# Paced splits of w_out, layer-norm statistics from sums and squares for three tiles, and a last unit in whole steps

## The chip, the cores and the metric

The kernel runs on one core of a Trainium2 chip. The metric is the device time of one launch in microseconds. TensorE multiplies matrices, VectorE and GpSimd work element by element, ScalarE applies functions, SyncE issues most of the loads. TensorE's clock has two levels, 1.2 and 2.4 GHz, and the profile gives the granted share of the higher one.

## The reference

One layer of a decoder trunk over 512 tokens of 1024 features, in float32. What matters here is the end of the first half and the second half:

```python
merged = sigmoid(mg_h) * (o_h @ w_br_hg) + sigmoid(mg_n) * (o_n @ w_br_nsa)
y = (1 + g1) * (merged @ w_out)
x = layer_norm(ALPHA * x + y) * ln1_g + ln1_b
h = layer_norm(x) * (1 + sc2) + sh2
y = (1 + g2) * hier_moe(h, ...)     # top-1 group of 4, top-2 of its 8 experts, 32 experts of 1024 x 512
x = layer_norm(ALPHA * x + y) * ln2_g + ln2_b
```

`layer_norm` takes the mean and the mean of the squared distances from it over the 1024 features of a token, with 1e-5 under the root.

## The kernel before

The 512 tokens are four tiles of 128. Until about 625 us the input projection, the two mixing branches and their gates are worked off. Every float32 matrix product there is made of three passes: each operand is split into a rounded high part and the rest (`wh` and `wl` of a weight, `mh` and `ml` of the merged activations), and high by high, high by low and low by high are summed in PSUM.

`run_jobs` (L332) goes through a list of jobs. A job has a weight block and a body that yields every few matmuls. At each yield the generator `ahead` (L336) is stepped once: it splits one piece of a coming block. `split1` issues for a piece the rounding on ScalarE (L279, `wh`) and the difference on VectorE (L281, `wl`); for the blocks of `w_out`, which are marked early, VectorE first scales the piece by 1 + g1 (L270). Each of the two `w_out` blocks is 512 columns wide and has four pieces. The block that is next is split first; of the three blocks after it, those marked early follow. Each engine works off its instructions in the order in which they were issued.

The jobs around the change are, in order: four blocks of `w_br_hg`, four of `w_br_nsa` (`br_job`, 256 columns each, 48 matmuls each into two PSUM tiles `pbr`), and the two of `w_out` for the first tile. For each `pbr` of `w_br_nsa` VectorE forms the gated sum (L1090, L1094), ScalarE rounds it (L1096, `mh`) and VectorE takes the rest (L1097, `ml`). There are eight of these groups, one for each 128 features of the merged activations.

`out_piece` (L1120) multiplies the merged activations of a tile by `w_out`, half a row at a time, adds ALPHA times the input row (L1126, `z`) and takes BN_STATS of the half (L1128). `ln` (L1199) then runs for each tile: BN_AGGR (L230) gives mean and variance, ScalarE's Ln and Exp (L232, L233) the reciprocal root `rs`; VectorE forms `acc` = (z - mean) x gain (L1207) and, by halves, `acc` x rs + bias (L1213) with BN_STATS of the result (L1214), from which a second BN_AGGR, Ln and Exp give the statistics `l2` of the norm ahead of the experts. TensorE transposes `z`, ScalarE copies it out (`zT`, L1222) and TensorE forms the router's logits from it (`plg`, L1194 and around). The router's choices on VectorE (`pk`, L1232 to L1262) lead to the ranks `prk` on TensorE and to the gather lists; the normed row `xh` (L1239) is split into `xhh` (L1242, ScalarE) and `xhl` (L1244, GpSimd for tiles 0 to 2; L1286, VectorE, within the last tile's gather). The work of the tiles is interleaved: each `yield` in `ln` is a due time for a planner that puts the next tile's `out_piece` in between. The last tile takes its BN_STATS in quarters and is ordered by hand.

The experts' weights come as 512 KB tiles `ew` on the queue of SyncE. L1315 issues them, each as its buffer comes free, in order. TensorE multiplies the gathered tokens (`p`, `py`, L182), and `pcb` (L180) adds the outcome back to the tokens' rows.

The last unit holds four experts side by side, each on 32 columns of TensorE. `half_up(h, py, ks)` issues the second product of half h of the output columns for the steps ks of the contraction, four instructions for each step. `weighted_halves` scales the product (L1541, `y`), rounds it (L1543, `yh`) and takes the rest (L1544, `yl`). `half_add` adds a tile's share to `acc` and sums the row (L1714); `squares` lets ScalarE sum the squares (L1697). `pl` spreads the gain and bias of the last norm over the partitions, ScalarE copies them out (L1737). Between the two halves' sums and the end stands `overflow`, a loop for tokens over an expert's 32 places that is not entered here, and a load of ScalarE's function table (L1749).

Of the kernel before, what the change touches and what calls it, by code (L numbers as in the profile page):

```python
# [26 lines left out]
AF = mybir.ActivationFunctionType  # L27
OP = mybir.AluOpType
# [39 lines left out]
LN_T, LN_P, LN_Q, LN_L, LN_R = 5000, 1500, 800, 0, 3500  # L68
MOD_F = 2
MOD_G = 2  # L70
SMALL = (8, 9)
# [68 lines left out]
def hybrid_kernel(ctx, tc, a, out, dbg=None, stop=None):  # L140
# [14 lines left out]
    def Q(name, dt=F32):  # L155
        return big.tile([128, 1024], dt, name=name, tag="Q", bufs=36)
# [163 lines left out]
    def run_jobs(jobs):  # L320
# [3 lines left out]
        def ahead(i):  # L324

            nb = [b for b in blocks[i + 1:] if b is not None]
            for b in nb[:1]:
                while len(b.w) < b.np:
                    b.fetch1()
                while len(b.h) < b.np and not b.raw:  # L330
                    b.split1()
                    yield  # L332
            for b in nb[1:4]:
                if b.early or b is nb[1]:
                    while len(b.w) < b.np:
                        b.fetch1()  # L336
                while b.early and len(b.h) < b.np:
                    b.split1()
                    yield
            while True:  # L340
                yield
# [778 lines left out]
    def out_piece(b, i, c, width):  # L1120

        z, n = zs[i], 256 if i + 1 == NT else 512
        py = PS("pyo")[:, 0:width]
        yield from proj_tok(b, py, i, mh, ml, width, c % 512)
        s_ = slice(c, c + width)
        V.scalar_tensor_tensor(z[:, s_], z[:, s_], ALPHA, py, op0=OP.mult, op1=OP.add)  # L1126
        for j in range(c // n, (c + width) // n):
            V.bn_stats(l1st[i][:, 6 * j:6 * j + 6], z[:, j * n:(j + 1) * n])  # L1128

# [58 lines left out]
    def logits_of(i):  # L1188
# [8 lines left out]
        return plg, lgT  # L1197

    def ln(i, z, st):  # L1199
        last = i == NT - 1  # L1200
        if last:
            tail_transposed()
            gather_first([0])
        mv, rs = layer_stats(z, "l1", st, later=True)
        ac = Q("acc")
# [5 lines left out]
        for half in range(2):  # L1211
            s_ = slice(half * 512, (half + 1) * 512)
            V.scalar_tensor_tensor(ac[:, s_], ac[:, s_], rs[:, 0:1], l1b[:, s_], op0=OP.mult, op1=OP.add)  # L1213
            V.bn_stats(st[:, half * 6:(half + 1) * 6], ac[:, s_])  # L1214
        mv2, rs2 = layer_stats(ac, "l2", st, later=True)
        if not last:
# [20 lines left out]

        xh = Q("xh")
        A.activation(xh.rearrange("p (k q) -> p q k", k=8), ac.rearrange("p (q k) -> p q k", k=8), AF.Identity,  # L1239
# [484 lines left out]
    py, py1 = PS("py"), PS("py")  # L1724
    for _ in half_up(0, py, range(4)):
        pass
    l2g, l2b = Q("l2g"), Q("l2b")
    pls = []
    for h_, l_ in zip(l2h, l2l):
        for s_ in halves_:  # L1730
            ps = PS("pl2")
            for j, x in enumerate((h_, l_)):
                mm(ps, oner, x[:, s_], j == 0, j == 1)
            pls.append(ps)
    y = weighted_halves(py, cs_, 0, 512)
    for j, ps in enumerate(pls):
        A.activation((l2g, l2b)[j // 2][:, halves_[j % 2]], ps, AF.Copy)  # L1737

    for x, _ in enumerate(half_up(1, py1, (0, 1))):
        if x < NT:  # L1740
            half_add(0, y, x)
    V.tensor_scalar(nsh, sums[:, :, 0], -1.0 / 512, None, op0=OP.mult)
    for _ in half_up(1, py1, (2, 3)):
        pass
    for i in range(NT):
        squares(i, 0)
    y = weighted_halves(py1, cs_, 512, 512)
    overflow()
    A.preload_act_table_set("natural_log_exp_and_others")  # L1749
    for i in range(NT):  # L1750
        half_add(1, y, i)
        squares(i, 1)
# [59 lines left out]
```

## Time and profile before

| | us |
|---|---|
| median of three runs | 1254.59 |
| the three runs | 1252.58 to 1255.31 |
| the profiled execution, whole time | 1251.85 |
| its span on the core | 1250.1 |
| TensorE busy in the span | 1171.4 (94%) |
| VectorE busy | 691.8 (55%) |
| ScalarE busy | 431.5 (35%) |
| GpSimd busy | 85.4 (7%) |

The times of the table and of the rows are of one profiled execution. Busy shares are means over stages with different limits: up to about 660 us TensorE is nearly always busy and the DMA engines little; from about 756 to 1217 us the DMA engines are; in between and behind, several engines wait for each other. Waits are given with what ended them. A line number is one of the kernel before; in the changed kernel the same statement stands 1 to 26 lines further down. Float32 matmuls are shown with their passes in some rows, so that 12 instructions can stand as 24.

### The profile page before, as it was taken

Reading aid. Unit: us, or ns where it says so; the run is one execution under the profiler, and the core shown is the slowest. Engines: PE = TensorE matmul, PEld = TensorE weight load, DVE = VectorE, ACT = ScalarE, POOL = GpSimd, SP = SyncE. Lnnn points to the kernel's source line nnn. Section 1 sums busy time; section 2 is a strip of 40 time slices with the busy share of each in tenths; the row PEclk is TensorE's granted clock in tenths of the full one; section 3 lists DMA queues with packets and bytes.
Section 4 is the critical chain, followed back from the end, with each engine's and each line's share of the span. In section 5 each row is a group of like instructions: output and inputs, shape, how many; then the busy total and the mean of one; then the engine's idle time right before and its main releaser. Section 6 shows DMA issues by size and latency. Waiting matters only on the chain. (4 is left out here: it accounts for less than half of the span.)

```text
span 1250.1 us, 18158 instructions
## 1 busy us (share of the span) xinstructions
PE 1171.4 (94%) x6455; PEld 803.1 (64%) x6455; DVE 691.8 (55%) x1626; ACT 431.5 (35%) x904; POOL 85.4 (7%) x164
## 2 busy tenths in 40 slices
PE   5999999899999999999998979999999899999986
PEld 4788898778888888878876763434435235455322
DVE  5564888787665665423495797535135134444314
ACT  4333656764444353555232341201102001112013
POOL 3011111121011011002000020000000000000000
PEclk9999999999999999999998989999999999999997
DMA  9954324134244244336255199999999999999991
GB/s 319 311 142 156 94 72 127 55 124 139 77 148 122 77 129 126 86 99 208 61 176 168 34 343 345 409 408 409 408 409 409 409 409 409 408 408 402 408 362 71
DMA packets 137629, 296.10 MB, mean 237 GB/s; under 512 B 11195, under 2 KB 74883, under 8 KB 137536
## 3 DMA queue, kind: packets, MB, share of 16 engines
q1 hardware_dynamic: 128224, 268.57, 58.9%
q0 software_dynamic: 8544, 23.97, 6.2%
q10 hardware_dynamic: 768, 2.37, 0.6%
q8 instruction: 52, 0.85, 0.3%
q14 instruction: 41, 0.34, 0.1%
HBM read 292.73 MB, written 4.76 MB: 238 GB/s over the span
## 5 line engine op out<-in xcount | busy, mean ns | idle before, releaser
L182 PE MATMUL p<-ew,xe 128*32 128x512 f32 (+1 forms) x960 | 195.6, 597 | 10.6 <-DMA ew<-in_exp_w_dram 10.1
L281 DVE TENSOR_TENSOR wl<-wst,wh 128x1024 fp32r<-128x1024 f32 (+1 forms) x93 | 109.6, 1201 | 75.4 <-ACT wh L279 74.5
L182 PEld LDWEIGHTS p<-ew,xe 128*32 128x32 f32 (+1 forms) x960 | 53.4, 122 | 146.1 <-issue 81.9
L182 PE MATMUL py<-ew,aT 128*32 128x512 f32 (+1 forms) x464 | 99.1, 598 | 8.8 <-DMA ew<-in_exp_w_dram 5.9
L1520 DVE TENSOR_TENSOR s<-s,p 128x512 f32<-128x512 f32 x13 | 8.9, 687 | 175.6 <-PE p L182 159.9
L279 ACT ACTIVATE wh<-wst 128x1024 fp32r<-128x1024 f32 (+1 forms) x94 | 93.9, 1031 | 32.7 <-DVE wst L270 20.2
L182 PEld LDWEIGHTS py<-ew,aT 128*32 128x32 f32 (+1 forms) x464 | 24.9, 121 | 73.6 <-issue 38.5
L1528 ACT ACTIVATE aT<-pat 128x512 f32<-128x512 f32 x13 | 7.8, 597 | 176.4 <-PE pat L186 176.4
L1569 DVE TENSOR_TENSOR acc<-acc,pcb 128x512 f32<-128x512 f32 x96 | 58.3, 681 | 8.3 <-PE pcb L180 8.3
L1543 ACT ACTIVATE yh<-y 128x512 fp32r<-128x512 f32 x26 | 16.4, 630 | 130.1 <-DVE y L1541 130.1
L180 PE MATMUL pgx<-pm,xhh 128*128 128x256 f32 (+1 forms) x224 | 55.6, 293 | 0.0
L180 PE MATMUL pgx<-pm,xhl 128*128 128x256 f32 (+1 forms) x224 | 54.1, 287 | 0.0
L1541 DVE SCALAR_TENSOR_TENSOR y<-py,cs,g2b 128x512 f32<-128x512 f32 x26 | 19.4, 748 | 58.5 <-PE py L182 58.3
L180 PE MATMUL pmg<-hh,wh 128*128 128x512 f32 x128 | 50.4, 394 | 0.0
L180 PE MATMUL psg<-hh,wh 128*128 128x512 f32 x128 | 50.3, 393 | 0.0
L180 PE MATMUL psg<-hl,wh 128*128 128x512 f32 x128 | 49.9, 390 | 0.0
L180 PE MATMUL psg<-hh,wl 128*128 128x512 f32 x128 | 49.9, 390 | 0.0
L180 PE MATMUL pmg<-hh,wl 128*128 128x512 f32 x128 | 49.8, 389 | 0.0
L180 PE MATMUL pmg<-hl,wh 128*128 128x512 f32 x128 | 49.8, 389 | 0.0
L180 PE MATMUL pcb<-yh,pT 128*128 128x512 f32 x104 | 44.0, 423 | 5.3 <-issue 5.3
L180 PEld LDWEIGHTS pgx<-pm,xhh 128*128 128x128 f32 x224 | 43.6, 197 | 8.0 <-issue 6.9
L519 POOL DMA_DIRECT2D adaw<-in_ada_w_dram x64 | 34.6, 542 | 193.4 <-PE ptp L186 40.2
(538 smaller groups left out, 2784.1 us busy)
## 6 DMA issues: line engine op xcount, KB each, us to landing
ew<-in_exp_w_dram SPq DMA_DIRECT2D x380, 512.0 KB, 10.1
wst<-in_w_in_dram SPq DMA_DIRECT2D x66, 512.0 KB, 4.8
adaw<-in_ada_w_dram POOLq DMA_DIRECT2D x64, 256.0 KB, 3.2
adaw<-in_ada_w_dram SPq DMA_DIRECT2D x16, 512.0 KB, 9.3
wst<-in_w_br_hg_dram SPq DMA_DIRECT2D x8, 512.0 KB, 6.8
wst<-in_w_br_nsa_dram SPq DMA_DIRECT2D x8, 512.0 KB, 3.6
wst<-in_w_out_dram SPq DMA_DIRECT2D x8, 512.0 KB, 6.7
ext_d<-ext_d POOLq DMA_DIRECT2D x1, 2560.0 KB, 17.1
```

The lines of the kernel that those rows point to most:

```text
L180: PE.matmul(o, l, r, start=start, stop=stop)
L182: PE.matmul(o, l, r, start=start, stop=stop, tile_position=pos)
L279: A.activation(wh, self.w[j], AF.Copy)
L281: (sub or V).tensor_sub(wl, self.w[j], wh.bitcast(F32))
L519: P_.dma_start(w, ada[:, k, 2048 + j * 512:2560 + j * 512])
L1520: V.tensor_mul(s1, s1, p3)
L1528: A.activation(aT, at_.rearrange("p (f s) -> p f s", f=4), AF.Copy)
L1541: V.scalar_tensor_tensor(y, py, cs_, g2b[c0 // 512][:, c0 % 512:c0 % 512 + n], op0=OP.mult, op1=OP.mult)
L1543: A.activation(yh, y, AF.Copy)
L1569: V.tensor_add(acc[i][:, s_], acc[i][:, s_], pc_)
```

## The change

There are three parts. First, `ahead` yields four times instead of once after each piece of an early block (`PACE = 4`), so that one piece of `w_out` is split in four steps. Second, for tiles 0 to 2 the statistics of both norms come from sums: L1126 and L1213 take an accumulated sum along with their result, a new `stats_of_sums` makes the mean of the two halves' sums on VectorE, and ScalarE takes the sum of the squares of mean - x over the whole row (its result goes to a buffer that later holds `xh`), then Ln and Exp. The last tile stays as it was. Third, in the last unit the steps run whole: the first half's steps 0 and 1, the eight `pl` with their copies, its steps 2 and 3, `weighted_halves`, then steps 0 and 1 of the second half, the four `half_add`, and steps 2 and 3 of the second half. Of the first half's squares only those of tiles 0 and 1 stay ahead of `yh`; those of tiles 2 and 3 follow behind the loop and the table load.

```diff
--- before.py
+++ after.py
@@ -67,6 +67,7 @@
 LOADS = [4, 4, 4, 4]
 LN_T, LN_P, LN_Q, LN_L, LN_R = 5000, 1500, 800, 0, 3500
 MOD_F = 2
+PACE = 4
 MOD_G = 2
 SMALL = (8, 9)
 PS_B = [0, 0]
@@ -336,7 +337,8 @@
                         b.fetch1()
                 while b.early and len(b.h) < b.np:
                     b.split1()
-                    yield
+                    for _ in range(PACE):
+                        yield
             while True:
                 yield
         for i, (b, body, pre) in enumerate(jobs):
@@ -1119,13 +1121,17 @@
 
     def out_piece(b, i, c, width):
 
-        z, n = zs[i], 256 if i + 1 == NT else 512
+        z = zs[i]
         py = PS("pyo")[:, 0:width]
         yield from proj_tok(b, py, i, mh, ml, width, c % 512)
         s_ = slice(c, c + width)
+        if i + 1 < NT:
+            V.scalar_tensor_tensor(z[:, s_], z[:, s_], ALPHA, py, op0=OP.mult, op1=OP.add,
+                                   accum_out=l1st[i][:, c // 512:c // 512 + 1])
+            return
         V.scalar_tensor_tensor(z[:, s_], z[:, s_], ALPHA, py, op0=OP.mult, op1=OP.add)
-        for j in range(c // n, (c + width) // n):
-            V.bn_stats(l1st[i][:, 6 * j:6 * j + 6], z[:, j * n:(j + 1) * n])
+        for j in range(c // 256, (c + width) // 256):
+            V.bn_stats(l1st[i][:, 6 * j:6 * j + 6], z[:, j * 256:(j + 1) * 256])
 
     jobs.append((None, spawn_job(lambda: x_rows(0))[1], None))
     jobs += [(wo[q], lambda b, q=q: out_piece(b, 0, q * 512, 512), None) for q in range(2)]
@@ -1196,12 +1202,24 @@
         A.activation(lgT, plg[:, 128:256], AF.Copy)
         return plg, lgT
 
+    def stats_of_sums(src, pre, st, junk):
+
+        mv, rs = small(pre + "mv", 2), small(pre + "rs", 2)
+        V.tensor_scalar(mv[:, 0:1], st[:, 0:1], st[:, 1:2], 1.0 / D, op0=OP.add, op1=OP.mult)
+        A.activation(junk, src, AF.Square, bias=mv[:, 0:1], scale=-1.0, accum_out=mv[:, 1:2])
+        A.activation(rs[:, 0:1], mv[:, 1:2], AF.Ln, bias=eps[:, 0:1], scale=1.0 / D)
+        A.activation(rs[:, 0:1], rs[:, 0:1], AF.Exp, scale=-0.5)
+        return mv, rs
+
     def ln(i, z, st):
         last = i == NT - 1
         if last:
             tail_transposed()
             gather_first([0])
-        mv, rs = layer_stats(z, "l1", st, later=True)
+            mv, rs = layer_stats(z, "l1", st, later=True)
+        else:
+            junk = Q("xh")
+            mv, rs = stats_of_sums(z, "l1", st, junk)
         ac = Q("acc")
         acc.append(ac)
         V.scalar_tensor_tensor(ac, z, mv[:, 0:1], l1g, op0=OP.subtract, op1=OP.mult)
@@ -1210,9 +1228,16 @@
         st = small("l2st", 12)
         for half in range(2):
             s_ = slice(half * 512, (half + 1) * 512)
-            V.scalar_tensor_tensor(ac[:, s_], ac[:, s_], rs[:, 0:1], l1b[:, s_], op0=OP.mult, op1=OP.add)
-            V.bn_stats(st[:, half * 6:(half + 1) * 6], ac[:, s_])
-        mv2, rs2 = layer_stats(ac, "l2", st, later=True)
+            if last:
+                V.scalar_tensor_tensor(ac[:, s_], ac[:, s_], rs[:, 0:1], l1b[:, s_], op0=OP.mult, op1=OP.add)
+                V.bn_stats(st[:, half * 6:(half + 1) * 6], ac[:, s_])
+            else:
+                V.scalar_tensor_tensor(ac[:, s_], ac[:, s_], rs[:, 0:1], l1b[:, s_], op0=OP.mult, op1=OP.add,
+                                       accum_out=st[:, half:half + 1])
+        if last:
+            mv2, rs2 = layer_stats(ac, "l2", st, later=True)
+        else:
+            mv2, rs2 = stats_of_sums(ac, "l2", st, junk)
         if not last:
             yield LN_T
             zT[i] = []
@@ -1235,7 +1260,7 @@
         V.scalar_tensor_tensor(lgi, rt[:, 1], mv2[:, 0:1], lgi, op0=OP.mult, op1=OP.add)
         V.scalar_tensor_tensor(lgi, lgi, rs2[:, 0:1], rt[:, 3], op0=OP.mult, op1=OP.add)
 
-        xh = Q("xh")
+        xh = Q("xh") if last else junk
         A.activation(xh.rearrange("p (k q) -> p q k", k=8), ac.rearrange("p (q k) -> p q k", k=8), AF.Identity,
                      bias=rs2[:, 1:2], scale=rs2[:, 0:1])
         th, tl = Q("xhh", F32R), Q("xhl", F32R)
@@ -1722,31 +1747,32 @@
         A.activation(h_, t, AF.Copy)
         V.tensor_sub(l_, t, h_.bitcast(F32))
     py, py1 = PS("py"), PS("py")
-    for _ in half_up(0, py, range(4)):
+    for _ in half_up(0, py, (0, 1)):
         pass
     l2g, l2b = Q("l2g"), Q("l2b")
-    pls = []
-    for h_, l_ in zip(l2h, l2l):
+    for t, h_, l_ in zip((l2g, l2b), l2h, l2l):
         for s_ in halves_:
             ps = PS("pl2")
             for j, x in enumerate((h_, l_)):
                 mm(ps, oner, x[:, s_], j == 0, j == 1)
-            pls.append(ps)
+            A.activation(t[:, s_], ps, AF.Copy)
+    for _ in half_up(0, py, (2, 3)):
+        pass
     y = weighted_halves(py, cs_, 0, 512)
-    for j, ps in enumerate(pls):
-        A.activation((l2g, l2b)[j // 2][:, halves_[j % 2]], ps, AF.Copy)
-
-    for x, _ in enumerate(half_up(1, py1, (0, 1))):
-        if x < NT:
-            half_add(0, y, x)
+    for _ in half_up(1, py1, (0, 1)):
+        pass
+    for i in range(NT):
+        half_add(0, y, i)
     V.tensor_scalar(nsh, sums[:, :, 0], -1.0 / 512, None, op0=OP.mult)
     for _ in half_up(1, py1, (2, 3)):
         pass
-    for i in range(NT):
+    for i in range(2):
         squares(i, 0)
     y = weighted_halves(py1, cs_, 512, 512)
     overflow()
     A.preload_act_table_set("natural_log_exp_and_others")
+    for i in range(2, NT):
+        squares(i, 0)
     for i in range(NT):
         half_add(1, y, i)
         squares(i, 1)
```

VectorE ahead of the split of the fourth `w_br_nsa` block, from the third of the eight groups of the merge, before; the last row is that split, the other L270 and L281 are of `w_out`'s pieces:

```order
L1090 TENSOR_TENSOR sgm<-sgm,pbr 128x512
L1094 TENSOR_TENSOR sgm<-sgm 128x512
L1097 TENSOR_TENSOR ml<-sgm,mh 128x512
L270 TENSOR_TENSOR wst<-wst,g1b 128x1024
L281 TENSOR_TENSOR wl<-wst,wh 128x1024 x2
L1090 TENSOR_TENSOR sgm<-sgm,pbr 128x512
L1094 TENSOR_TENSOR sgm<-sgm 128x512
L1097 TENSOR_TENSOR ml<-sgm,mh 128x512
L281 TENSOR_TENSOR wl<-wst,wh 128x1024 x2
```

And after, from the same group (L270, L281 and L1090 to L1097 are now L271, L282 and L1092 to L1099); the second and third of the three L282 are the fourth block's split:

```order
L1092 TENSOR_TENSOR sgm<-sgm,pbr 128x512
L1096 TENSOR_TENSOR sgm<-sgm 128x512
L1099 TENSOR_TENSOR ml<-sgm,mh 128x512
L271 TENSOR_TENSOR wst<-wst,g1b 128x1024 x2
L282 TENSOR_TENSOR wl<-wst,wh 128x1024
L1092 TENSOR_TENSOR sgm<-sgm,pbr 128x512
L1096 TENSOR_TENSOR sgm<-sgm 128x512
L1099 TENSOR_TENSOR ml<-sgm,mh 128x512
L271 TENSOR_TENSOR wst<-wst,g1b 128x1024
L282 TENSOR_TENSOR wl<-wst,wh 128x1024 x3
L271 TENSOR_TENSOR wst<-wst,g1b 128x1024
L282 TENSOR_TENSOR wl<-wst,wh 128x1024
```

Counted over the whole order from the L281 that stands at 634.51 in the trace (it is the same in both) to the fourth block's split, there were 16 instructions of L270 and L281 and four groups; now there are 13 and four. The three that are missing, for pieces of `w_out`, follow behind the split, ahead of and between the next groups.

VectorE in the first tile's `ln`, from the first norm's statistics, before (`l1st` and `l2st` hold the statistics or sums, `l1mv` and `l2mv` the means):

```order
L230 BN_AGGR l1mv<-l1st 128x2
L1207 SCALAR_TENSOR_TENSOR acc<-z,l1mv,l1g 128x1024
L1213 SCALAR_TENSOR_TENSOR acc<-acc,l1rs,l1b 128x512
L1214 BN_STATS l2st<-acc 128x6
L1213 SCALAR_TENSOR_TENSOR acc<-acc,l1rs,l1b 128x512
L1214 BN_STATS l2st<-acc 128x6
L230 BN_AGGR l2mv<-l2st 128x2
```

And after:

```order
L1208 TENSOR_SCALAR l1mv<-l1st 128x1
L1225 SCALAR_TENSOR_TENSOR acc<-z,l1mv,l1g 128x1024
L1235 SCALAR_TENSOR_TENSOR acc,l2st<-acc,l1rs,l1b 128x512 x2
L1208 TENSOR_SCALAR l2mv<-l2st 128x1
L1129 SCALAR_TENSOR_TENSOR z,l1st<-z,pyo 128x512
```

The BN_STATS and BN_AGGR are gone, and the mean stands where BN_AGGR stood.

ScalarE in the second tile, from the scaling of the first tile's row, before:

```order
L1245 ACTIVATE acc<-acc 128x1024
L232 ACTIVATE l1rs<-l1mv,eps 128x1
L233 ACTIVATE l1rs<-l1rs 128x1
L232 ACTIVATE l2rs<-l2mv,eps 128x1
L233 ACTIVATE l2rs<-l2rs 128x1
L1118 DMA z<-in_x_dram 128x1024
L1222 ACTIVATE zT<-pzT 128x512 x2
```

And after (L1209 is the square, which writes to the buffer of `xh`):

```order
L1270 ACTIVATE acc<-acc 128x1024
L1209 ACTIVATE xh,l1mv<-z,l1mv 128x1024
L1210 ACTIVATE l1rs<-l1mv,eps 128x1
L1211 ACTIVATE l1rs<-l1rs 128x1
L1209 ACTIVATE xh,l2mv<-acc,l2mv 128x1024
L1210 ACTIVATE l2rs<-l2mv,eps 128x1
L1211 ACTIVATE l2rs<-l2rs 128x1
L1120 DMA z<-in_x_dram 128x1024
L1247 ACTIVATE zT<-pzT 128x512 x2
```

Two squares of 1024 elements are new, each ahead of a Ln and Exp, and both ahead of the copies `zT`.

TensorE in the last unit, from the last `pl`, before:

```order
L180 MATMUL pl_10683<-l2bh,oner 128x512
L180 MATMUL pl_10683<-l2bl,oner 128x512
L182 MATMUL py<-ew,aT 32x512
L180 MATMUL pcb<-yh,pT 128x512
L180 MATMUL pcb<-yl,pT 128x512
L182 MATMUL py<-ew,aT 32x512
```

And after:

```order
L181 MATMUL pl_10672<-l2bh,oner 128x512
L181 MATMUL pl_10672<-l2bl,oner 128x512
L183 MATMUL py<-ew,aT 32x512 x16
L181 MATMUL pcb<-yh,pT 128x512
L181 MATMUL pcb<-yl,pT 128x512
L181 MATMUL pcb<-yh,pT 128x512
```

Before, one `py` and a pair of `pcb` alternate four times, and 12 `py` follow; now 16 `py` stand together (steps 2 and 3 of the first half and 0 and 1 of the second), then the four pairs of `pcb`, then 8 `py`. The `pl` stood behind all 16 `py` of the first half and stand behind the first 8 now.

## Rows read from the trace of the kernel before

**Rows 1.** Table by stretch: start:end, busy time of each engine, granted clock, DMA share, GB/s.
```profile
664.00:668.00 4.00, 3.29 (x7) 2.19 (x8) 3.71 (x5) 1.56 (x2) 0.00 (x0) 0.50 0.55 172
734.00:738.00 4.00, 3.43 (x29) 3.13 (x30) 3.79 (x11) 2.58 (x4) 3.37 (x3) 1.00 0.93 280
746.00:750.00 4.00, 3.35 (x16) 3.35 (x16) 3.50 (x12) 1.87 (x2) 0.00 (x0) 0.50 1.03 412
800.00:900.00 100.00, 96.23 (x539) 45.84 (x537) 36.99 (x84) 15.52 (x30) 0.00 (x0) 1.00 1.03 409
1217.00:1221.00 4.00, 4.00 (x10) 0.87 (x8) 1.96 (x6) 0.00 (x0) 0.00 (x0) 1.00 0.07 26
```

**Rows 2.** Waits, 684 to 760: engine, line, waited for: us in all, times, longest.
```profile
PE prk L180 <- DVE pk L1261: 7.1, 2, 5.0
PE plg L182 <- ACT zT L1222: 2.7, 2, 1.5
...
SPq L1315 <- DVE xhl L1286: 7.5, 1, 7.5
```

**Rows 3.** Timeline of TensorE: start, duration, line, out<-in [idle before <-releaser].
```profile
664.67 0.80 PE L180 MATMUL pbr<-onh,wh 128*128 128x512 f32 x1 [5.32 <-ACT wh L279]
...
665.93 0.80 PE L180 MATMUL pbr<-onh,wl 128*128 128x512 f32 x1
...
668.81 0.39 PE L180 MATMUL pbr<-onh,wh 128*128 128x512 f32 x1
```

**Rows 4.** Timeline of VectorE ahead of the fourth `w_br_nsa` block.
```profile
634.51 1.22 DVE L281 TENSOR_TENSOR wl<-wst,wh 128x1024 fp32r<-128x1024 f32 x1
...
637.93 0.68 DVE L1090 TENSOR_TENSOR sgm<-sgm,pbr 128x512 f32<-128x512 f32 x1
...
640.64 1.22 DVE L270 TENSOR_TENSOR wst<-wst,g1b 128x1024 f32<-128x1024 f32 x1
...
664.65 2.36 DVE L281 TENSOR_TENSOR wl<-wst,wh 128x1024 fp32r<-128x1024 f32 x2 [0.25 <-ACT wh L279]
```

**Rows 5.** Timeline of VectorE in the `ln` stage, tiles 0, 1 and 2.
```profile
690.42 1.28 DVE L1207 SCALAR_TENSOR_TENSOR acc<-z,l1mv,l1g 128x1024 f32<-128x1024 f32 x1
...
704.22 0.68 DVE L1126 SCALAR_TENSOR_TENSOR z<-z,pyo 128x512 f32<-128x512 f32 x1
...
705.91 2.27 DVE L1207 SCALAR_TENSOR_TENSOR acc<-z,l1mv,l1g 128x1024 f32<-128x1024 f32 x1
708.28 0.75 DVE L1213 SCALAR_TENSOR_TENSOR acc<-acc,l1rs,l1b 128x512 f32<-128x512 f32 x1
...
735.56 1.49 DVE L1279 TENSOR_SCALAR lk<-pos 128x2 f32<-128x2 f32 x1
```

**Rows 6.** Timeline of GpSimd in the `ln` stage.
```profile
704.69 2.40 POOL L1244 TENSOR_TENSOR xhl<-xh,xhh 128x1024 fp32r<-128x1024 f32 x1 [125.25 <-ACT xhh L1242]
...
734.63 2.40 POOL L1244 TENSOR_TENSOR xhl<-xh,xhh 128x1024 fp32r<-128x1024 f32 x1 [12.37 <-ACT xhh L1242]
```

**Rows 7.** Timeline of ScalarE in the `ln` stage, tile 1.
```profile
711.42 0.30 ACT L232 ACTIVATE l2rs<-l2mv,eps 128x1 f32<-128x1 f32 x1 [4.98 <-DVE l2mv L230]
...
712.13 1.08 ACT L1222 ACTIVATE zT<-pzT 128x512 f32<-128x512 f32 x2 [0.18 <-issue]
```

**Rows 8.** Timeline of TensorE in the tail.
```profile
1221.68 2.78 PE L182 MATMUL py<-ew,aT 128*32 128x512 f32 x24
```

**Rows 9.** Timeline of VectorE in the tail.
```profile
1216.87 0.69 DVE L1714 CUSTOM_DVE_ANT_0 acc<-acc,pcb 128x512 f32<-128x512 f32 x1 [1.53 <-PE pcb L180]
...
1224.53 0.75 DVE L1541 SCALAR_TENSOR_TENSOR y<-py,cs,g2b 128x512 f32<-128x512 f32 x1 [1.84 <-PE py L182]
```

**Rows 10.** Timeline of ScalarE in the tail.
```profile
1225.98 0.61 ACT L1543 ACTIVATE yh<-y 128x512 fp32r<-128x512 f32 x1
...
1231.76 0.72 ACT L1697 ACTIVATE sq<-acc,nsh 128x512 f32<-128x512 f32 x1 [2.54 <-DVE sums L1714]
1232.39 0.19 ACT L1697 ACTIVATION_READ_ACCUMULATOR sq<-acc,nsh 128x1 f32 x1
```

## The prediction

> **What bounds the kernel now.** I read the table by stage first. From 800 to 900 us the DMA engines are full (share 1.03, 409 GB/s) [rows 1]: the expert weights stream in, TensorE waits only for them, and work on the other engines costs nothing there. Whatever moves the stream as a whole moves the end by as much. So the second view is what holds the stream back: the queue that issues it stands 7.5 us for `xhl` at L1286, the gather of the last tile, which hangs on TensorE and VectorE before it [rows 2]. Time lost by TensorE between the branch projections and that gather is therefore lost at the end, one for one. Third, the timelines of that stretch. Between 659 and 665 TensorE has one stall, of 5.32 us, in front of the fourth `w_br_nsa` block [rows 3], and behind it, from 664 to 668, a granted clock of 0.50 [rows 1]. In the `ln` stage it waits twice, 2.7 us together, for `zT` [rows 2]. The tail after the stream is the third place.
>
> **Part 1, the paced splits.** The stall ends at 664.67 with `wh` of the fourth block; the third matmul, at 665.93, needs its `wl`, which VectorE makes from 664.65 [rows 3, 4]. VectorE is late because it works without a gap: an L281 or an L270 takes 1.14 us from start to start (three from 634.51 to 637.93), a group of L1090, L1094, L1097, with its wait for `mh`, 2.71 us (637.93 to 640.64) [rows 4]. By the order, from the instruction at 634.51 to the fourth block's split there stand 16 of the first kind and 4 groups now, 13 and 4 after: three instructions for pieces of `w_out` move behind the split. Counted: 16 x 1.14 + 4 x 2.71 = 29.1, so 663.6, where the trace has 664.65; 1.1 us is small waits. After: 13 x 1.14 + 10.8 = 25.7, so the split starts between 660.2 and 661.3, and the third matmul runs 3.4 to 4.5 us earlier. The first two matmuls need `wh` alone, and ScalarE has no piece of `w_out` ahead of it there any more, so they run in the stall. To this comes the clock. From 665.93 to 668.81 stand eight matmuls, seven steps [rows 3]; at 0.23 us, the usual step (2.78 / 12 in [rows 8]), these would take 1.6, they took 2.9: 1.3 us lost to a clock of 1.2 instead of 2.4 GHz after an idle time of 5.32. What is left of the stall runs from 659.35 (664.67 - 5.32) to at most 661.4 or 662.5, with two matmuls in it: some 2 us idle. For `pk` TensorE waits twice, 2.1 and 5.0 us [rows 2]; the granted clock was 1.00 behind the first, from 734 to 738, and 0.50 behind the second, from 746 to 750 [rows 1]. The 2 us that are left resemble the first, so I take it that the clock holds. Gain 4.7 to 5.8, I take 5.3.
>
> What is late next: the last group of the merge. After the split VectorE has one more split, an L270 and two L281, and four groups: 660.2 + 2 x 1.14 + 3 x 1.14 + 4 x 2.71 = 676.7, or 677.8 with the small waits. TensorE, 5.3 us earlier, needs that last `ml` at about 677; so it is just in time, and a gain beyond 5.8 is not to be had. The third block's split is also behind paced pieces now, but by the same count it is no later than before. The loads on the queue of SyncE keep their order, and the buffers they wait for come free earlier. The edit adds no instruction.
>
> **Part 2, the statistics.** VectorE loses the BN_STATS and BN_AGGR of three tiles and gets two 128x1 instructions for the means, and accumulating forms; ScalarE gets two Squares of 1024 for each tile. TensorE waits for `zT` in tiles 1 and 2, and `zT` stands in ScalarE's queue behind Ln and Exp of `l2`, so this chain is the one that counts. Before, for tile 1: `z` at 704.22, L1207 from 705.91, L1213 from 708.28, Ln at 711.42, `zT` at 712.13 [rows 5, 7]. L1207 took 2.27 us there and 1.28 in tile 0 [rows 5]; in tile 1 it ends at 708.18, 1.09 after the end of GpSimd's L1244 (704.69 + 2.40 = 707.09) [rows 6]. I read this as VectorE being held until GpSimd is through. So the earlier start that the missing BN_STATS and BN_AGGR give it is worth nothing: L1207 still ends at 708.2. The mean's instruction now stands ahead of it. No row has it, but one of its kind: L1279, on 128x2, took 1.49 us and ended at 737.05, with GpSimd's next L1244 (734.63 + 2.40 = 737.03) [rows 5, 6]. By that row the mean is held. The Trainium skill, GPSIMD Engine Reference, section Specifications, names as the forms that contend for the shared SBUF interfaces those in a 2-port mode or with two SBUF inputs; a mean over one operand would go free by it, and the sum would be -6.9; L1279, also of one tensor, speaks against that. Held, the chain is: mean at 707.1; Square 1.35 (0.82 from the start of a Square of 512 to the end of its read-out, and half of the 1.08 of two `zT` for 512 more) [rows 7, 10]; Ln and Exp 0.7 (711.42 to 712.13); L1213's successor at 709.1, 0.8 later than before. From there two accumulating instructions of 0.75, a mean of 0.2, Square 1.35 and 0.7: 712.9 against 712.13. So 0.8 us lost in tile 1 and again in tile 2, 1.6 in all; tile 0 shows no wait of TensorE for `zT`. If the mean is not held, Square starts at 705 to 706, Exp is through before L1207 ends, and the loss is 0 to 0.4 in all. A gain is excluded by L1207's end. I take 1.6, by L1279.
>
> The other unknown is the accumulating form with two operands from SBUF. The nearest row accumulates a 128x512 sum with one operand from PSUM, in 0.69 us, no slower than without [rows 9]. At half rate L1213's successor would take some 1.28 instead of 0.75: 0.53 x 2 in each of two tiles, 2.1 us more. The Trainium skill, Vector Engine (DVE) Microarchitecture Reference, section Points that are easy to get wrong, says that this instruction with two SBUF sources that aren't bf16 runs at half throughput, no port being left for the accumulator's readback. L1207's 1.28 us for 1024 elements, without an accumulator, does not show it; no row here has it with one. By that page the change would bring 3.4 us instead of 5.5.
>
> **Part 3, the tail.** Now four single `py` instructions, each with a pair of `pcb` behind it, stand ahead of the last 12 (24 passes in the trace), which take 2.78 from 1221.68, to 1224.46 [rows 8]. What of this is needed: from 1217 to 1221 only 26 GB/s arrive (share 0.07) [rows 1], about 100 KB, and the instructions at 1221.68 wait for no DMA. So the last weights are there between 1221 and 1221.7. The eight broadcasts of `ln2` move into waits of TensorE for weights, and their copies fill an idle ScalarE: nothing. The four pairs of `pcb` no longer sit between single instructions. After the last weights at least five, at most eight instructions are left, 0.23 us each (2.78 / 12): 1.2 to 1.85, so TensorE ends between 1222.2 and 1223.5; I take 1223.2, a gain of 1.2. Then `yh`: `y` is ready at 1225.28 (1224.53 + 0.75) [rows 9], but ScalarE starts `yh` at 1225.98, behind four squares [rows 10]; with two it is free in time: 0.7 more. The two squares moved behind the loop cost 1.8 in ScalarE's idle 2.54 [rows 10], nothing. Gain 1.8; from 0.6 (squares alone) to 2.9.
>
> **Sum.** -5.3 + 1.6 - 1.8 = -5.5 us. The profiled execution took 1251.85, so 1246.35; it lies 2.74 under the median of the runs, 1254.59, and the same distance gives 1249.1.
>
> **The rivals.**
> The clock falls all the same: two short matmuls do not break the idle time. Then part 1 brings 3.4 to 4.5, I take 3.7, and the time is 1250.7. For it speaks that the chain could end at 662.5, which leaves 2.9 us less two matmuls, more than any row that held; against it the 2.1.
> Half rate: 2.1 more, 1251.2.
> The mean is not held: part 2 costs 0.2, 1247.7.
> The gain of part 1 is not carried on, because the gather at L1286 or the first expert weights are bound by something that keeps its time: only the tail and part of the statistics count, about 1253.5. Against it: between 680 and the gather TensorE and VectorE take turns without a load among their long waits.
> Slower than before: the chain through ScalarE is longer than counted, place tiles 1 and 2. If forms at half rate, the held mean and also `z` with an accumulator (0.68 to 1.28) come together in one chain, it grows by 2.5 us for each tile; TensorE's waits of about 1.3 become 3.8, near the 5.0 after which the clock fell, and each fall costs 1.3 to 1.9: (2.5 + 1.7) x 2 = 8.4 against 7.1 of gain, so 1255.9. It decides from 3.55 us for each tile.
>
> **How the numbers follow.** Chances: forecast 0.43, mean not held 0.1, clock 0.17, half rate 0.12, not carried on 0.08, slower 0.1. The likeliest gives 1249.1, by itself 1248 to 1250.5. Range: low with part 1 at 5.8, the mean free and the tail at 2.9, 1246.1; high with the clock's fall, half rate and the tail at 0.6 together, 1254.0; outside lie the slower case and some of the extremes. A measurement tells about 0.2%, 2.5 us, from nothing: faster needs less than 1252.1. That is nearly all of the forecast and of the free mean, most of the clock's and half rate's cases: 0.71; slower, over 1257.1, is the larger half of the slower case, 0.07; within 0.2% the rest, 0.22.
>
> **What would show it.** Right: the wait for the fourth block's `wl` near 2 us, with matmuls at 0.23 us behind it; `ml` of the last group around 677; the mean of tile 1 ending with L1244; `zT` 0.8 later after the tile's `z` than before; `yh` directly behind `y`; the last `py` about 1.2 us nearer to the stream's end. Wrong: slow matmuls behind that wait, an accumulating instruction of 1.2 us, or `xhl` at L1286 that has not moved.

## The result and the profile after

| | before | after |
|---|---|---|
| median of six runs each, us | 1253.70 | 1247.61 |
| range of the runs | 1252.58 to 1255.31 | 1245.63 to 1249.17 |
| ratio, 95% interval | | 0.9949, 0.9938 to 0.9961 |
| profiled execution, whole time | 1251.85 | 1247.05 |
| its span | 1250.1 | 1245.3 |

The change makes the kernel faster by about 6.1 us (0.9949 of 1253.7 gives 6.4, the medians 6.1); run twice more later, it came to 0.9946 (0.9933 to 0.9959) and 0.9956 (0.9943 to 0.9969). The forecast was 5.5 less, 1249.1, with 1246.1 to 1254.0 around it. The total was right; two of the three terms were not.

The best view for a change that moves things along one chain is a table of stations, read from the two timelines:

| station | before | after | moved |
|---|---|---|---|
| first wait of the `w_br_nsa` blocks, ahead of the change | 626.57 | 626.24 | -0.33 |
| fourth block's third matmul (first that needs `wl`) | 665.93 | 661.24 | -4.69 |
| `zT` of tile 1 | 712.13 | 706.25 | -5.88 |
| `zT` of tile 2 | 727.01 | 720.99 | -6.02 |
| `xhl` of the last tile | 748.65 | 742.58 | -6.07 |
| first expert matmul `p` | 752.41 | 747.28 | -5.13 |
| last `p` that waits for weights | 1199.76 | 1194.83 | -4.93 |
| last `py` ends | 1224.46 | 1218.78 | -5.68 |
| `yl` of the second half | 1226.63 | 1220.27 | -6.36 |
| first `pcb` behind the loop | 1229.77 | 1224.11 | -5.66 |
| first `pcl` with `dg` | 1237.71 | 1232.11 | -5.60 |
| span | 1250.1 | 1245.3 | -4.8 |

The first row is not the change: the 14 profiled executions of these kernels, those of the experiments below included, differed by up to 1.7 us (626.14 to 627.84) before anything that was edited. So below, a time is measured from that first wait, or from the station before it.

The stall, which answers to [rows 3, 4]. First the table by stretch of the changed kernel (start:end, busy time of each engine, granted clock, DMA share, GB/s):

```profile
657.00:661.00 4.00, 2.69 (x11) 1.60 (x9) 3.92 (x4) 3.84 (x5) 0.00 (x0) 1.00 0.00 0
661.00:665.00 4.00, 3.77 (x17) 3.12 (x18) 4.00 (x5) 0.00 (x0) 0.00 (x0) 1.00 0.63 186
```

TensorE in its timeline (start, duration, line, out<-in, idle before and what ended it):

```profile
659.00 0.50 PE L181 MATMUL pbr<-onh,wh 128*128 128x512 f32 x1
659.33 0.40 PE L181 MATMUL pbr<-onl,wh 128*128 128x512 f32 x1
661.24 0.50 PE L181 MATMUL pbr<-onh,wl 128*128 128x512 f32 x1 [1.50 <-DVE wl L282]
661.57 0.40 PE L181 MATMUL pbr<-onh,wh 128*128 128x512 f32 x1
```

VectorE in its timeline:

```profile
657.69 1.22 DVE L271 TENSOR_TENSOR wst<-wst,g1b 128x1024 f32<-128x1024 f32 x1
658.83 3.49 DVE L282 TENSOR_TENSOR wl<-wst,wh 128x1024 fp32r<-128x1024 f32 x3
...
676.23 0.69 DVE L1099 TENSOR_TENSOR ml<-sgm,mh 128x512 fp32r<-128x512 f32 x1 [0.70 <-ACT mh L1098]
```

Of the three L282 from 658.83, 1.14 us apart, the second and third are the fourth block's, so its split starts at 660.0 instead of 664.65. The first two matmuls run at 659.00 and 659.33, in the stall, and 1.50 us of waiting are left where 5.32 stood. The granted clock stays at 1.00 in both stretches; before it was 0.50 from 664 to 668 [rows 1]. The last `ml` runs from 676.23 to 676.92.

The statistics, which answer to [rows 5 to 7]. The changed kernel's timeline of VectorE in tile 1:

```profile
698.47 0.68 DVE L1129 SCALAR_TENSOR_TENSOR z<-z,pyo 128x512 f32<-128x512 f32 x1
699.08 0.09 DVE L1129 DVE_READ_ACCUMULATOR z<-z,pyo 128x1 f32 x1
699.20 0.21 DVE L1208 TENSOR_SCALAR l1mv<-l1st 128x1 f32<-128x1 f32 x1
699.45 2.99 DVE L1225 SCALAR_TENSOR_TENSOR acc<-z,l1mv,l1g 128x1024 f32<-128x1024 f32 x1
702.54 0.75 DVE L1235 SCALAR_TENSOR_TENSOR acc<-acc,l1rs,l1b 128x512 f32<-128x512 f32 x1
703.22 0.08 DVE L1235 DVE_READ_ACCUMULATOR acc<-acc,l1rs,l1b 128x1 f32 x1
```

GpSimd at the same time:

```profile
698.94 2.41 POOL L1269 TENSOR_TENSOR xhl<-xh,xhh 128x1024 fp32r<-128x1024 f32 x1 [119.87 <-ACT xhh L1267]
```

ScalarE, from the square of the second norm:

```profile
704.26 1.16 ACT L1209 ACTIVATE xh<-acc,l2mv 128x1024 f32<-128x1024 f32 x1 [2.76 <-DVE l2mv L1208]
705.32 0.18 ACT L1209 ACTIVATION_READ_ACCUMULATOR xh<-acc,l2mv 128x1 f32 x1
...
706.25 1.08 ACT L1247 ACTIVATE zT<-pzT 128x512 f32<-128x512 f32 x2 [0.18 <-issue]
```

Every accumulating instruction takes what it took without the sum (0.68 and 0.75) and a read-out of 0.08. The mean, L1208, takes 0.21 us while GpSimd works (698.94 to 701.35); L1225 takes 2.99 and ends 1.09 after GpSimd, as L1207 did. From `z` to `zT` it is 7.78 us here and was 7.91 (704.22 to 712.13).

The waits of TensorE in the changed kernel, 677 to 760, which answer to [rows 2] (us in all, times, longest):

```profile
PE prk L181 <- DVE pk L1286: 5.5, 2, 3.4
PE plg L183 <- ACT zT L1247: 2.4, 2, 1.4
```

And its table by stretch there:

```profile
728.00:732.00 4.00, 3.48 (x19) 3.30 (x19) 3.79 (x11) 2.65 (x4) 3.41 (x4) 0.67 1.02 383
740.00:744.00 4.00, 3.41 (x17) 3.41 (x17) 3.46 (x11) 1.80 (x2) 0.00 (x0) 0.50 1.02 412
```

The two waits for `zT` are 0.3 us shorter together. After the wait of 2.12 us for `pk` the clock fell in this execution (0.67 from 728 to 732; 1.00 at the same place before), and behind the second it stayed at 0.50 for longer: from `xhl` to the first `p` it took 4.70 us, before 3.76. Over all 14 profiles this way took 2.52 and 2.53 us in the two whose clock stood at 1.00 all along it, and 3.63 to 4.70 in the twelve others, whose mean clock there was 0.59 to 0.77. The table by stretch of one of the two, the kernel with eight yields and the squares ahead (below), where `xhl` starts at 741.46 and `p` at 743.98:

```profile
740.00:744.00 4.00, 3.97 (x36) 3.65 (x35) 3.02 (x9) 1.42 (x3) 0.00 (x0) 1.00 1.04 407
```

The same kernel run again took 4.54 us there, at a mean clock of 0.62. So the clock in the gather moves a single execution by up to 2 us, and one pair of profiles doesn't measure the change.

The tail, which answers to [rows 8 to 10]. The changed kernel's timeline of TensorE:

```profile
1216.88 1.90 PE L183 MATMUL py<-ew,aT 128*32 128x512 f32 x10 [0.24 <-SPq L1615]
1224.11 0.80 PE L181 MATMUL pcb<-yh,pT 128*128 128x512 f32 x1 [5.32 <-ACT sq L1722]
```

VectorE:

```profile
1218.83 0.75 DVE L1566 SCALAR_TENSOR_TENSOR y<-py,cs,g2b 128x512 f32<-128x512 f32 x1 [1.80 <-PE py L183]
...
1220.91 0.06 DVE L1601 MEMSET ocnt<- 128x1 f32 x1
```

ScalarE:

```profile
1219.61 0.63 ACT L1568 ACTIVATE yh<-y 128x512 fp32r<-128x512 f32 x1 [0.89 <-DVE y L1566]
1221.58 1.28 ACT L1773 ACT_TABLE_LOAD   x1 [1.34 <-DVEq L1615]
1222.87 0.72 ACT L1722 ACTIVATE sq<-acc,nsh 128x512 f32<-128x512 f32 x1
...
1224.35 0.19 ACT L1722 ACTIVATION_READ_ACCUMULATOR sq<-acc,nsh 128x1 f32 x1
```

`yh` starts as soon as `y` is ready. But the first `pcb` starts 3.20 us behind the loop's MEMSET (1220.91 to 1224.11), where before it was 2.50 (1227.27 to 1229.77), and the two moved squares stand behind the table load at just that place.

### The profile page after: what moved, and what is told of

Same layout as the page of the kernel before. It is cut to its first block, busy times and chain, and to the rows that moved or that the text cites. A ratio compares the mean times of both kernels' runs of the same rounds, so it can differ in the third digit from the quotient of the medians.

```text
span 1245.3 us, 18172 instructions
## 1 busy us (share of the span) xinstructions
PE 1169.0 (94%) x6455; PEld 802.1 (64%) x6455; DVE 685.0 (55%) x1626; ACT 438.4 (35%) x916; POOL 82.8 (7%) x164
## 3 DMA queue, kind: packets, MB, share of 16 engines
q10 hardware_dynamic: 768, 2.37, 0.6%
## 5 line engine op out<-in xcount | busy, mean ns | idle before, releaser
L282 DVE TENSOR_TENSOR wl<-wst,wh 128x1024 fp32r<-128x1024 f32 (+1 forms) x93 | 109.3, 1201 | 74.2 <-ACT wh L280 73.4
L183 PEld LDWEIGHTS py<-ew,aT 128*32 128x32 f32 (+1 forms) x464 | 24.8, 121 | 74.7 <-issue 37.0
```

The source lines that it names most:

```text
L183: PE.matmul(o, l, r, start=start, stop=stop, tile_position=pos)
L282: (sub or V).tensor_sub(wl, self.w[j], wh.bitcast(F32))
```

## The experiments

Three kernels apply one part each to the kernel before.

**The paced splits alone.** The loop `for _ in range(PACE): yield` and `PACE = 4`, nothing else.

> The kernel before with the paced splits alone. Theory: the stall ahead of the fourth w_br_nsa block falls from 5.3 us to about 1.5, the matmuls behind it run at 0.23 us, and the time falls by about 5.5 us. If the statistics carry part of the whole gain of 6.1 us (they end the wait for zT 0.1 us sooner), it falls by 5 or less; if the clock still falls behind the shorter stall, by about 4.

Measured: 1247.75 us against 1253.34, ratio 0.9942 (0.9923 to 0.9961). The waits of TensorE in this kernel, 655 to 760:

```profile
PE prk L181 <- DVE pk L1263: 7.1, 2, 5.0
PE plg L183 <- ACT zT L1224: 2.7, 2, 1.5
PE pbr L181 <- DVE wl L282: 1.5, 1, 1.5
```

And the matmuls behind the stall, in its timeline:

```profile
662.82 0.50 PE L181 MATMUL pbr<-onh,wl 128*128 128x512 f32 x1 [1.50 <-DVE wl L282]
663.16 0.39 PE L181 MATMUL pbr<-onh,wh 128*128 128x512 f32 x1
```

The stall is 1.50 us, the clock holds, and the waits of the statistics are those of before. Measured from the first wait (627.84 here), the first `p` (748.14) has moved by 5.5 us and the end of the span (1246.0) by 5.4. So this part alone gives what the whole change gives, as far as the times can tell, and it gives about the 5.3 that was forecast for it.

**The statistics alone.** `stats_of_sums` and the accumulating forms, nothing else.

> The kernel before with the statistics from sums alone. Theory from the trace of the changed kernel: the mean's instruction is not held by GpSimd, the accumulating forms cost 0.75 and 0.69 us, TensorE's waits for zT shrink by 0.1 to 0.15 us each in tiles 1 and 2, the stall of 5.3 us stays: 0 to -0.5 us, no change that can be told. The prediction's account gave +1.6, half rate +3.7.

Measured: 1254.02 us, ratio 1.0005 (0.9993 to 1.0016). The stall of 5.3 us is back and the wait for `zT` is 0.3 shorter, by the waits of TensorE, 655 to 760:

```profile
PE prk L181 <- DVE pk L1285: 5.9, 2, 3.8
PE pbr L181 <- ACT wh L280: 5.3, 1, 5.3
PE plg L183 <- ACT zT L1246: 2.4, 2, 1.4
```

The time speaks against a loss of 3.7 us, but its interval reaches to +2.0, so it does not tell 1.6 from nothing; the waits do, for they did not grow. In the profiles the gain is a steady 0.3: the two waits for `zT` take 2.37 to 2.42 us together in the eight profiles with this part as it is, and 2.66 to 2.67 in the four without it. In two profiles whose clock held behind the stall, from the third matmul of the fourth block to the `zT` of tile 2 it takes 60.04 us with the paced splits alone (662.82 to 722.86) and 59.75 in the changed kernel (661.24 to 720.99).

**The tail alone.** The last unit's whole steps, nothing else.

> The kernel before with the last unit's whole steps alone. Theory: py ends 0.75 us nearer to the last weights, yh no longer waits behind squares (0.7), and 0.7 is given back behind the loop, where the first pcb starts 3.2 us after the loop's last instruction instead of 2.4: about -0.8 us. If the late pcb is an accident of that one execution, -1.4; the prediction's account gave -1.8.

Measured: 1252.9 us, ratio 0.9992 (0.9980 to 1.0004); the time alone tells neither -0.8 nor -1.8 from nothing. VectorE's `yl` and MEMSET in this kernel's timeline:

```profile
1227.59 0.69 DVE L1544 TENSOR_TENSOR yl<-y,yh 128x512 fp32r<-128x512 f32 x1 [0.69 <-ACTq L1590]
1228.24 0.06 DVE L1576 MEMSET ocnt<- 128x1 f32 x1
```

TensorE's first `pcb` behind the loop:

```profile
1231.41 0.80 PE L180 MATMUL pcb<-yh,pT 128*128 128x512 f32 x1 [5.30 <-ACT sq L1697]
```

The `pcb` is 3.17 us behind the MEMSET, so the loss is no accident of one execution.

**The squares put back.** The changed kernel with all four squares ahead of `yh`:

```diff
-    for i in range(2):
+    for i in range(NT):
         squares(i, 0)
...
-    for i in range(2, NT):
-        squares(i, 0)
```

> The changed kernel with the squares of tiles 2 and 3 put back ahead of yh. If the two squares behind the table load are what holds the first pcb back by 0.7 us, pcb starts again 2.4 us behind the loop's last instruction, yh waits 0.7 us for ScalarE, and the time is the same within 0.2 us as the changed kernel's (about -6.1 against before). If the late start has nothing to do with the squares, pcb stays 3.2 us behind and the time is 0.7 us longer than the changed kernel's (about -5.4).

Measured: 1247.34 us, ratio 0.9948 (0.9926 to 0.9969). The same two of VectorE in its timeline:

```profile
1220.86 0.69 DVE L1569 TENSOR_TENSOR yl<-y,yh 128x512 fp32r<-128x512 f32 x1 [1.40 <-ACTq L1615]
1221.50 0.06 DVE L1601 MEMSET ocnt<- 128x1 f32 x1
```

And TensorE's first `pcb`:

```profile
1224.30 0.80 PE L181 MATMUL pcb<-yh,pT 128*128 128x512 f32 x1 [5.62 <-issue]
```

The `pcb` stands 2.80 us behind the MEMSET, between the two expected values. Over all profiles of this study the way from `yl` to `pcb` took 3.00 to 3.54 us with the squares ahead (seven profiles, 3.14 in before's) and 3.64 to 4.06 with them behind (seven, three of them of the changed kernel). The two ranges do not overlap. So the squares behind the loop cost 0.6 us in the mean (3.84 against 3.19), most of the 0.7 that `yh` gains. Why TensorE starts later when ScalarE has more to do there, no run settles: in the profile its start is put down to the first of these squares, which its data do not need.

**The mean on two columns.** What decides whether GpSimd holds the mean:

```diff
-        V.tensor_scalar(mv[:, 0:1], st[:, 0:1], st[:, 1:2], 1.0 / D, op0=OP.add, op1=OP.mult)
+        V.tensor_scalar(mv[:, 0:2], st[:, 0:2], st[:, 1:2], 1.0 / D, op0=OP.add, op1=OP.mult)
```

> The changed kernel with the mean's instruction on two columns instead of one (the second is overwritten by the square's sum). L1208 took 0.21 us beside GpSimd's L1269 on 128x1, where the 128x2 of L1304 took 1.47 and ended with GpSimd. If two elements for each partition make the instruction one that GpSimd holds, L1208 of tiles 1 and 2 ends with L1269 (1.5 to 2.2 us), the square starts then, and zT comes about 0.8 us later than in the changed kernel, as the prediction had it. If something else held L1304, L1208 stays at 0.2 us and nothing moves.

Measured in one run, whose time tells nothing by itself: 1249.69 us. VectorE in tile 1, in this kernel's timeline:

```profile
700.03 2.17 DVE L1208 TENSOR_SCALAR l1mv<-l1st 128x2 f32<-128x2 f32 x1
702.24 1.28 DVE L1225 SCALAR_TENSOR_TENSOR acc<-z,l1mv,l1g 128x1024 f32<-128x1024 f32 x1
```

GpSimd there:

```profile
699.77 2.40 POOL L1269 TENSOR_TENSOR xhl<-xh,xhh 128x1024 fp32r<-128x1024 f32 x1 [119.67 <-ACT xhh L1267]
```

And TensorE's wait for `zT`:

```profile
708.45 1.15 PE L183 MATMUL plg<-zT,pk 128*64 128x128 f32 x16 [2.11 <-ACT zT L1247]
```

With two columns L1208 takes 2.17 us and ends with GpSimd (699.77 + 2.40 = 702.17); in tile 2 it takes 2.19, and 0.23 where GpSimd is idle. L1225 behind it is back at 1.28. TensorE waits 2.11 us instead of 1.39, and in tile 2 1.72 instead of 0.99: 0.7 us each against the changed kernel. The prediction's 0.8 was counted against the kernel before; against that it is 0.6 each (1.52 and 1.14 there). So its chain was right, and a little too long; what it took for granted, that one column behaves as two, was wrong.

**The low part on VectorE.** `xhl` of tiles 0 to 2 is made by VectorE, ahead of the next `z`, and GpSimd has nothing to do there:

```diff
-        if not last:
-            P_.tensor_sub(tl, xh, th.bitcast(F32))
...
+            V.tensor_sub(tl, xh, th.bitcast(F32))
             yield LN_R
```

> The changed kernel with the low part xhl of tiles 0 to 2 made on VectorE instead of GpSimd. If it is GpSimd's L1269 that stretches L1225 of tiles 1 and 2 to 2.95 and 2.99 us, L1225 takes 1.28 there and L1304 of tile 2 takes 0.17 instead of 1.47; VectorE pays about 1.2 us for each tile, so zT comes at most 0.5 us sooner and the time changes by less than 1 us. If L1225 is slow for another reason, it stays near 3 us.

Measured: 1244.97 us, ratio 0.9952 (0.9934 to 0.9970), the same as the changed kernel. VectorE in tile 1, in its timeline:

```profile
698.78 1.23 DVE L1289 TENSOR_TENSOR xhl<-xh,xhh 128x1024 fp32r<-128x1024 f32 x1 [0.32 <-ACT xhh L1267]
...
700.65 0.21 DVE L1208 TENSOR_SCALAR l1mv<-l1st 128x1 f32<-128x1 f32 x1
700.90 1.28 DVE L1225 SCALAR_TENSOR_TENSOR acc<-z,l1mv,l1g 128x1024 f32<-128x1024 f32 x1
```

L1225 takes 1.28 without GpSimd beside it. So it was GpSimd's instruction that stretched it; VectorE pays 1.23 for `xhl` instead, and TensorE waits 0.3 us longer for `zT` in each tile (1.69 and 1.27).

**Eight yields.** `PACE = 8` in the changed kernel.

> The changed kernel with eight yields for each piece. By the order, eight instead of 13 instructions of L271 and L282 stand ahead of the fourth block's split, and one piece of w_out behind the last group. If what is left of the stall (1.5 us) is still VectorE being late, it is gone, and the time falls by another 1 to 1.5 us unless the last ml is then late for the first w_out matmuls; then part of it is a wait there. If the stall of 1.5 us has another cause, it stays.

Measured: 1245.02 us, ratio 0.9944 (0.9929 to 0.9958). The one new wait among TensorE's, 655 to 760:

```profile
PE pyo L181 <- ACT mh L1098: 0.5, 1, 0.5
```

And where it stands in the timeline:

```profile
675.17 0.50 PE L181 MATMUL pyo<-wh,mh 128*128 128x512 f32 x1 [0.52 <-ACT mh L1098]
```

The wait for `wl` is gone, and 0.52 us of it come back at the first `w_out` matmuls, which wait for the last `mh`. `zT` of tile 2 comes at 719.92 instead of 720.99. Three more kernels were run beside each other, and two of them again:

> The changed kernel once more, beside the next two. Theory: about -6 us against before, the wait ahead of the fourth block's wl 1.5 us, as in the three profiles that had it. If its gain was helped by the chip that it ran on, it lies nearer to -4.8, the difference of the two profiled executions.

> The changed kernel with eight yields for each piece and all four squares ahead of yh. Theory: the paced splits are nearly all of the gain; the wait of 1.5 us is gone and about 0.5 of it comes back at the first w_out matmul, so it lies 1.0 us under the changed kernel. The squares give 0.7 at yh and take 0.4 behind the loop, so that their place is worth 0.3 at most. If the eighth yield moves nothing that the end sees, it equals the changed kernel.

> The kernel before with eight yields for each piece and nothing else. Theory: statistics and tail together bring 0.5 to 1 us by their traces, so this lies 0.5 to 1 us above the run with eight yields and both. If the two other parts bring nothing that the end sees, it equals that run.

> The kernel with eight yields and the squares ahead of yh once more, since its interval and that of the changed kernel overlapped. If the 1.0 us of the removed wait is real, its ratio lies 0.001 under the changed kernel's in the next run again; if the difference was chance, the two ratios agree within 0.0005.

> The changed kernel beside the run with eight yields: about -6 us against before, ratio 0.995, and 1.0 us or more above the other.

| kernel | median, us | ratio to before | 95% interval |
|---|---|---|---|
| changed, again | 1247.16 | 0.9946 | 0.9933 to 0.9959 |
| eight yields, squares ahead | 1244.51 | 0.9933 | 0.9917 to 0.9949 |
| before with eight yields only | 1246.37 | 0.9936 | 0.9923 to 0.9948 |
| eight yields, squares ahead, again | 1247.24 | 0.9950 | 0.9937 to 0.9964 |
| changed, a third time | 1248.39 | 0.9956 | 0.9943 to 0.9969 |

The kernel with eight yields and the squares ahead lay under the changed one in both pairs, by 0.0013 and 0.0006, 0.8 to 1.6 us. The intervals overlap, and the second difference lies next to the 0.0005 that was set for chance, not at the 0.001 set for a real gain; the first pair's profiled execution with eight yields (1242.62) is also one of the two with the full clock in the gather. The timeline shows 1 us less to the end of the statistics; that it reaches the end is not shown. With eight yields, the two other parts (with the squares ahead) are worth nothing that the times tell (0.9936 against 0.9933).

The changed kernel's profiles also held a surprise. In the two later ones the clock fell behind the same wait of 1.50 us; the table by stretch of the first of them:

```profile
657.00:661.00 4.00, 2.87 (x12) 1.73 (x10) 3.77 (x4) 3.98 (x5) 0.00 (x0) 1.00 0.00 0
661.00:665.00 4.00, 3.62 (x9) 2.86 (x10) 4.00 (x5) 0.00 (x0) 0.00 (x0) 0.58 0.63 185
```

There it cost 1.5 us: from the third matmul (661.38) to the `zT` of tile 1 (707.89) it took 46.51 us, where the first profile took 45.01 (661.24 to 706.25).

## Why the prediction was right, point by point

**What bounds the kernel**: right. What TensorE gained at the fourth block stood at the last `xhl` (-6.07), and the stream moved with the first `p` (-5.13 and -4.93). Of the 1.1 us between `xhl` and the stream 0.9 fall between `xhl` and `p`, with the lower clock there (0.59 in the mean against 0.77 before); with the paced splits alone this way took 3.65 us.

**Part 1**: right, in size and in mechanism: 5.3 was forecast, 5.4 measured by itself. The count of instructions gave a split between 660.2 and 661.3; it came at 660.0 (660.3 from the first wait's shift), without the small waits. The last group was put at 676.7 to 677.8 and ended at 676.92, in time: TensorE did not wait for it. That a gain beyond 5.8 is not to be had did not hold: with eight yields alone `zT` of tile 1 came 78.98 us behind the first wait, before 85.56, which is 6.6 less. And one step was lucky: that the clock holds behind the wait that is left, as it did behind the 2.1 us for `pk`. Behind 1.50 us it held in five of seven profiles and fell in two, both of the changed kernel, which has three; behind the 2.1 us itself, at 1.00 in the row that the step was read from, it fell in nine of 14. So the rival of the falling clock was not refuted; it is what some executions do. It named a gain of 3.7 for that case, 1.6 less, and 1.5 was measured.

**Part 2**: wrong. The term of +1.6 measured -0.3. The step that failed is "by that row the mean is held": the row had two columns, the mean has one, and the run with two columns shows that this makes the difference (0.21 against 2.17 us). The trace of before also had a row that spoke the other way, the BN_AGGR that the mean replaces, another form, on two columns, beside GpSimd's `xhl` of 704.69 to 707.09:

```profile
705.67 0.21 DVE L230 BATCH_NORM_AGGREGATE l1mv<-l1st 128x2 f32<-128x12 f32 x1
```

The rival "the mean is not held" was the right case, at a chance of 0.1, and its time, 1247.7, is close to the 1247.61 measured; in part by chance, since its gain was 6.9 and 6.1 came. It counted 0.2 of cost where 0.3 were won: "A gain is excluded by L1207's end" failed too. L1225 does end as long after GpSimd as L1207 did, but from there to `zT` it takes 3.81 us instead of 3.95 (702.44 to 706.25, 708.18 to 712.13). The Trainium skill, GPSIMD Engine Reference, section Specifications, names instructions in a 2-port mode and those with two SBUF inputs; it does not say that one operand goes free, which is what the prediction drew from it. The number of operands does not decide here: the mean has one tensor operand in both runs, and it went free on one column and was held on two. Half rate did not come: 0.75 us with the sum and 0.75 without. So the sentence of the Trainium skill, Vector Engine (DVE) Microarchitecture Reference, section Points that are easy to get wrong, does not hold for these instructions, and the measurement decides. The reading that L1207 ends 1.09 after GpSimd was right (1.09 again), and the low part on VectorE shows it by its absence.

**Part 3**: half right. `yh` gained its 0.7: from the end of the last `py` to `yl` it takes 1.49 us instead of 2.17. From the last `p` that waits to the end of the last `py` the old tail took 24.70 us in the profile of before and 24.13 to 25.58 in the three others that have it, 24.8 in the mean; the new one took 23.95 here and 23.89 to 24.00 in the nine others: 0.8 in the mean (0.1 to 1.7 by single profiles), where 1.2 was forecast. "Nothing" for the two squares behind the loop failed: their cover, ScalarE's idle time, was there, but TensorE started later all the same, and 0.6 us were given back. In all about 0.9 instead of 1.8, too little for the times to tell.

**The sum**: -5.5 stood against -5.4 - 0.3 - 0.9 = -6.6 by the profiles and -6.1 by the medians. It was near because one term was 1.9 us too dear and another 0.9 too good, which partly cancelled, and because the term that counts was right; the cancelling is luck. The time of 1247.61 lies 1.5 us under the forecast of 1249.1, and 0.9 of that is that the kernel before came to 1253.70 over six runs, not to the 1254.59 of three that the forecast started from. The profiled pair shows 4.8: it began 0.3 ahead, and lost 0.9 in the gather and 0.8 in the last `pcl` (6.58 us for eight where 5.77 were before, at a mean clock of 0.56 against 0.64), which makes that one execution a poor measure of the change.

## What to carry to other kernels

Where an in-order engine is late for one consumer, count the instructions ahead of the late one in the built order, before and after, and multiply by the pitch in the trace: here that gave a 5 us gain to within a few tenths, where the clock held. A row that is to price a new instruction must match it in shape too, down to one column or two. Work that is moved into an engine's idle time must be checked for who waits for that engine's progress, not only for how much idle time there is.

## What the runs showed of the hardware

- VectorE's tensor-by-scalar instruction on 128x1 took 0.21 us beside GpSimd's tensor-by-tensor `xhl`, on 128x2 2.17 us, until GpSimd was through (0.23 with GpSimd idle). The scalar-tensor-tensor on 128x1024 ended 1.07 to 1.09 us after GpSimd in all 24 places of the profiles where the two ran at once (2.27, 2.29 us before; 2.99, 2.95 after; 1.28 with GpSimd idle).
- A scalar-tensor-tensor with two float32 operands from SBUF and an accumulated sum took 0.75 us for 512 elements, as without, and 0.08 for the read-out.
- The same idle time of TensorE was not always followed by the same clock. Behind 1.50 us it stayed at 1.00 in five profiles of seven and fell in two; behind 1.9 to 2.1 us, at the first wait for `pk`, it fell in nine of 14; behind 3.4 to 3.8 us, at the second, in seven of eight; behind 5.0 to 5.3 us it fell in all eight cases.
